# Two transformer layers on one core: row steps at five seams issued as a pipeline over token tiles, and one product cut in halves

## The chip, the core and the metric

The kernel runs on one core of a Trainium2 chip. A core has five engines that run side by side and meet only at semaphores: TensorE (PE, matrix products), VectorE (DVE), ScalarE (ACT), GpSimd (POOL) and SyncE (SP), whose queue issues nearly all of this kernel's transfers. SBUF is the working memory, PSUM the accumulator of PE. The metric is the device time of one execution in microseconds (us), the median over the timed executions. Below, "tile" with a number is one of the eight blocks of 128 tokens (tile 0 to tile 7).

## What is computed

Two layers on 1024 tokens of width 1024, all in fp32. Cut to what the change touches:

```python
# first layer, after its attention and recurrence
mix = concat([y_att, y_rwkv]) @ w_out                      # seam A
x   = x + g_m * rms_norm(mix, mix_post_norm)
hf  = rms_norm(x, ffn_pre_norm) * (1 + sc_f) + sh_f
f   = (silu(hf @ w_ffn_gate) * (hf @ w_ffn_up)) @ w_ffn_down
x   = x + g_f * rms_norm(f, ffn_post_norm)                 # seam B
# second layer
u   = rms_norm(x, g_mix_pre);  z = u @ w_in                # seam B, its end
mixed = sigmoid(gate_a) * ya + sigmoid(gate_b) * (ob @ w_b_out)
h   = x + rms_norm(mixed @ w_o, g_mix_post)                # seam C
u2  = rms_norm(h, g_ffn_pre)                               # seam C, its end
f   = (gelu(conv(u2 @ w_ffn_up)) * ...) @ w_ffn_down
h   = h + rms_norm(f, g_ffn_post)                          # seam D
g   = sigmoid(h @ w_ple_gate)
h   = h + rms_norm(e * g, g_ple_post)                      # seam E
```

rms_norm divides each token's row by the root of the mean of its squares and multiplies by a gain.

## The kernel before

Every fp32 operand of a product is kept as a high and a low part (the low one is a subtraction on DVE or POOL, called a split here), and a product takes three matmuls (`mm3`, three lines of the profile: L105 to L107 in the plain products, L288 to L290 in the feed-forward ones). Operands of products lie with the model width on the partitions, so a token row that was normalized has to be transposed by PE before the next product. The feed-forward products use seven products in place of eight for a two by two block, so the transposed rows of two token tiles are also combined into sums (`put_pair`, which ends with the transposes, ACT copies and some nine DVE operations for a pair of tiles).

A **seam** is the place where one big product ends and the next begins. There each of the eight token tiles goes through row steps of 1024 columns: sum of squares on ACT (L119), the reciprocal root on POOL (two tiny operations, L114 and L115, tile `rs_y`), the scaling by root and gain on DVE (`scalar_tensor_tensor`, L530 in `post_add`, L541 in `renorm`), the residual add on DVE (L531), a store of the new residual to DRAM, then the second norm in the same way, and the transposes with their copies and splits (L154 or the lines of `put_pair`).

- **Seam A** (`mo2`): the second half (k 0 to 3) of w_out's product, added by DVE (L1928) to a first half that was stored in DRAM earlier (`half_d`), then the row steps and `put_pair`.
- **Seam B** (`done1`): row steps after the last products of the first w_ffn_down; `done` is called for the even tiles between the last product and its sum into `acc` (L468), for the odd ones after it.
- **Seam C** (`mo3`, `mo4`): four blocks `ob` are made (load `yl`, multiply by `yr` on DVE L2020, split on ACT and POOL L215; `yl` and `yr` have one buffer each), eight feature blocks are made from them (`fm`, DVE product L2028, POOL add L2029 with a loaded `ma`, one buffer), then the whole product with w_o, eight rows of weights, for each token tile, and the row steps.
- **Seam D** (`done2`): as B after the second w_ffn_down, without the second norm. The weights of w_ple_gate are loaded behind the stores of x1d, since SP issues in order.
- **Seam E** (`pl`): the product with w_ple_gate and the last norm.

The program is written as Python loops, but the order in which an engine runs its instructions is not that of the text alone: the tile framework's scheduler (switched on by one argument at the kernel's end) gives each engine its own order by modelled times, and the semaphores follow. So some work of neighbouring token tiles already overlaps in the kernel before.

Of the kernel before, what the change touches and what calls it, by code (L numbers as in the profile page):

```python
# [8 lines left out]
FP = mybir.dt.float32  # L9
# [15 lines left out]
class Core:  # L25
# [84 lines left out]
    def rsqrt(self, x, n, scale, eps):  # L110

        nc = self.nc
        y = self.small.tile([128, n], FP, name="rs_y", tag=f"rs_y{n}")
# [104 lines left out]
class Ops:  # L218
# [28 lines left out]
    def put_pair(self, c, g, xe, xo):  # L247

        nc = c.nc
        raw = lambda: c.t2([128, 4, 128])  # L250

        def tr(x, q):
            ps = c.psum([128, 4, 128], "tr")
            for k in range(4):
                nc.tensor.transpose(ps[:, k], x[:, (4 * q + k) * 128:(4 * q + k + 1) * 128], c.ident)
            return ps

        def put(s, x, eng):
# [19 lines left out]
        put(self.S1, s1, nc.vector)  # L278
        put(self.S3, s3, nc.gpsimd)
        put(self.S2, a11, nc.vector)  # L280
        put(self.S4, a12, nc.gpsimd)


def mm7(c, out, pairs, start, stop):
# [112 lines left out]
def down7(c, ap, rings, fd, w, nk, done):  # L397
# [56 lines left out]
    ops = ahead(operands(), c.nah)  # L454
    bank = lambda: [c.psum([128, 2, 512]) for _ in range(2)]

    def mul(ps, start, *to, between=None):
        n, s, t = next(ops)
        for g in range(4):
            gs = slice(128 * g, 128 * g + 128)  # L460
            mm7(c, ps[g // 2][:, g % 2], [((s[:, 0, j, gs], s[:, 1, j, gs]), (t[:, 0, j], t[:, 1, j])) for j in range(n)], start, True)
        if between is not None:
            between()
        for e, h in to:
            for q in range(2):
                d = acc[:, 2 * q:2 * q + 2, e, 512 * h:512 * h + 512]
                if (e, h) in first:
                    nc.vector.tensor_add(d, d, ps[q])  # L468
                else:
                    nc.scalar.activation(d, ps[q], AF.Copy)  # L470
            first.add((e, h))

    for n in range(len(groups)):
        pa, pb = bank(), bank()
# [3 lines left out]
        mul(pb, False, (0, 1))  # L478
        mul(pa, False, (1, 1))
        mul(bank(), True, (0, 0))  # L480
        mul(pa, False, (1, 0), between=None if n < len(groups) - 1 else
            lambda: [done(i, acc[:, i // 2, 0]) for i in range(0, NT, 2)])
    for i in range(1, NT, 2):
        done(i, acc[:, i // 2, 1])


class Rings:
# [31 lines left out]
    return {name: cols[:, s] for name, s in at.items()}  # L519


def post_add(c, ap, y, x, G, out, t=None):

    nc = c.nc
    ss = c.small.tile([128, 1], FP, name="ss", tag="ss")
    c.sumsq(y, ss, ap.tile([128, D], BF, name="sqj", tag="sqj", bufs=1))
    r = c.rsqrt(ss, 1, 1.0 / D, EPS)
    if t is None:
        t = ap.tile([128, D], FP, name="pa", tag="s4", bufs=c.n4)
# [4 lines left out]
def renorm(c, ap, x, i, act, g, b=None):  # L534

    nc = c.nc
    ss = c.small.tile([128, 1], FP, name="ss", tag="ss")
    c.sumsq(x, ss, ap.tile([128, D], BF, name="sqj", tag="sqj", bufs=1))
    r = c.rsqrt(ss, 1, 1.0 / D, EPS)
# [1243 lines left out]
def two_layers(ctx, tc, *args):  # L1783
# [91 lines left out]
    with pool("mo") as ap:  # L1875
# [14 lines left out]
        def prologue():  # L1890
# [4 lines left out]
                features(k)  # L1895
                yield
            for i in range(NT):
                for hf in range(2):
                    sl = slice(hf * 512, hf * 512 + 512)
                    t = ap.tile([128, 512], FP, name="hm", bufs=2)  # L1900
                    ps = c.psum([128, 512])
                    c.mm3(ps, [((h.tok(k, 0, i), h.tok(k, 1, i)), (wt[k - 4][:, 0, sl], wt[k - 4][:, 1, sl])) for k in range(4, 8)])
                    nc.scalar.activation(t, ps, AF.Copy)
                    nc.sync.dma_start(half[i * 128:i * 128 + 128, sl], t)
                    yield
# [11 lines left out]
        c.wlayout()  # L1917
    at.__exit__(None, None, None)
    c.layout(ps=(2, 2), tr=(1, 4))
    with pool("mo2") as ap:  # L1920
# [3 lines left out]
        get, get_h = loader(ap, x_in), loader(ap, half, "ht", 2)  # L1924
        for i in range(NT):
            ps = row_product(c, h, wt, i, range(4))
            y = get_h(i)
            nc.vector.tensor_add(y, y, ps)  # L1928
            xt = get(i)
            post_add(c, ap, y, xt, G1, xt, y)  # L1930
            store(x1d, i, xt)
            xn = renorm(c, ap, xt, i, None, Gh, Bh)
            if i % 2:
                h.put_pair(c, i // 2, xe, xn)
            xe = xn
    wp.__exit__(None, None, None)
    fd = tc.dram_tile([22, 128, T], FP, name="f_d")
    c.layout(ps=(1, 8))
# [16 lines left out]
    with Down(c, pool, "d1") as dn:  # L1955
# [3 lines left out]
        def done1(i, y):  # L1959
# [5 lines left out]
            _, G2, Gu = h  # L1965
            with c.after():
                xt = get(i)
            post_add(c, dn.ap, y, xt, G2, y, y)
            store(x2d, i, y)
            h[0].put_T(c, i, renorm(c, dn.ap, y, i, None, Gu), "ps")  # L1970
        dn.run(fd, p["w_ffn_down"], done1)
    h = h[0]
    c.layout(ps=(2, 3), tr=(1, 2))
# [33 lines left out]
    c.layout(ps=(2, 3), tr=(1, 2))  # L2007
    hp = pool("hp2")
    h = Ops(hp.__enter__(), "h2")
    wp = ctx.enter_context(ExitStack())  # L2010
    woa = wp.enter_context(pool("woa"))
    wt = rows_w(c, woa, p["w_o_2"], range(3), "woa")
    with pool("mo3") as ap:
        ob = []
        for k in range(4):
            t = ap.tile([128, T], FP, name="yl", bufs=1)
            nc.sync.dma_start(t, obd[k])
            r = ap.tile([128, T], FP, name="yr", bufs=1)
# [12 lines left out]
    c.n4 = 3
    c.wlayout()
    c.layout(ps=(2, 2), tr=(1, 4))
    wob = wp.enter_context(pool("wob"))
    c.wlayout(2)
    wt += rows_w(c, wob, p["w_o_2"], range(3, 8), at={7: h.free(3)})
    c.wlayout()
    with pool("mo4") as ap:
        G3, Gh = row_bcast(c, ap, p["g_mix_post_2"], "G3"), row_bcast(c, ap, p["g_ffn_pre_2"], "Gh2")
        c.tp, c.nt2 = ap, 5  # L2040
        get = loader(ap, x2d)
        for i in range(NT):
            ps = row_product(c, h, wt, i)
            xt = get(i)
            post_add(c, ap, ps, xt, G3, xt)
            store(h1d, i, xt)
            xn = renorm(c, ap, xt, i, None, Gh)
            if i % 2:
                h.put_pair(c, i // 2, xe, xn)
            xe = xn  # L2050
    wp.close()
    fd = tc.dram_tile([22, 128, T], FP, name="f2_d")
    c.layout(ps=(1, 8))
    c.wlayout(4, 7)
# [7 lines left out]
    with Down(c, pool, "d2") as dn:  # L2062
# [3 lines left out]
        def done2(i, y):  # L2066
# [14 lines left out]

    c.layout(ps=(2, 4))
    c.wlayout(3, 1)
    c.n4 = 6
    with pool("pl") as ap:
        G5 = row_bcast(c, ap, p["g_ple_post_2"], "G5")
        get, get_e = loader(ap, x1d), loader(ap, ed)
        wt = rows_w(c, ap, p["w_ple_gate_2"], range(8))
        for i in range(NT):
            ps = row_product(c, h, wt, i)  # L2090
            g = ap.tile([128, D], FP, name="pg", tag="s4", bufs=c.n4)
# [4 lines left out]
            post_add(c, ap, g, xt, G5, xt, g)  # L2096
            store(out, i, xt)
    c.wlayout()
    hp.__exit__(None, None, None)

# [23 lines left out]
```

## Time and profile before

| what | value |
|---|---|
| timed executions | 3799.55, 3803.8, 3804.47 us, median 3803.8 us |
| profiled execution | 3812.14 us, of which the profile's span is 3810.3 us |
| mean granted TensorE clock | 0.862 of full speed |
| busy shares of the span | PE 86%, DVE 61%, POOL 40%, ACT 38% |

The profiled execution is one more run of the same program; times of stages are taken from it. A busy share says how long an engine had an instruction in flight, averaged over stages with different limits. Of the granted clock there are two levels, full (2.4 GHz, shown as 1.00) and half (1.2 GHz, 0.50); a stretch shows the mean of what it had.

### The profile page before, as it was taken

Reading aid. Unit: us, or ns where it says so; the run is one execution under the profiler, and the core shown is the slowest. Engines: PE = TensorE matmul, PEld = TensorE weight load, DVE = VectorE, ACT = ScalarE, POOL = GpSimd, SP = SyncE. Lnnn points to the kernel's source line nnn. Section 1 sums busy time; section 2 is a strip of 40 time slices with the busy share of each in tenths; the row PEclk is TensorE's granted clock in tenths of the full one; section 3 lists DMA queues with packets and bytes.
Section 4 is the critical chain, followed back from the end, with each engine's and each line's share of the span. In section 5 each row is a group of like instructions: output and inputs, shape, how many; then the busy total and the mean of one; then the engine's idle time right before and its main releaser. Section 6 shows DMA issues by size and latency. Waiting matters only on the chain.

```text
span 3810.3 us, 42512 instructions
## 1 busy us (share of the span) xinstructions
PE 3273.1 (86%) x15652; PEld 2637.0 (69%) x15652; DVE 2313.9 (61%) x3405; ACT 1430.9 (38%) x2433; POOL 1515.3 (40%) x1217
## 2 busy tenths in 40 slices
PE   3778767998996869999886999989978899998888
PEld 2666545676774658887675788777856688886767
DVE  5569977657643465454898110016743688888983
ACT  3345433333333243333433221136632444444332
POOL 3114345424323244443874322131133354547851
PEclk7888865556567879999997999999989899999989
DMA  5552232212123432222332222220043222213234
GB/s 172 151 167 79 85 122 67 73 39 63 36 68 119 153 105 84 83 83 71 114 125 75 80 58 89 87 77 10 7 133 138 89 83 83 83 61 138 101 138 148
DMA packets 262655, 356.15 MB, mean 93 GB/s; under 512 B 17599, under 2 KB 194720, under 8 KB 261424
## 3 DMA queue, kind: packets, MB, share of 16 engines
q1 hardware_dynamic: 261392, 353.21, 28.6%
q8 instruction: 123, 2.02, 0.2%
q14 instruction: 84, 0.69, 0.1%
q0 software_dynamic: 1056, 0.23, 0.0%
HBM read 257.36 MB, written 96.02 MB: 93 GB/s over the span
## 4 chain that ended last, share of the span: by engine, by line
PE 48%; POOL 4%; DVE 4%; DMA 4%; issue 2%; ACT 2%; SPq 0%; POOLq 0%; ACTq 0%; DVEq 0%
PE ps L288 9%; PE ps L290 9%; PE ps L289 9%; PE ps L106 5%; PE ps L105 5%; PE ps L107 5%; POOL op L437 2%; POOL sm L429 1%; DMA raw<-f_d 1%; DVE sm L429 1%; PE o L578 1%; PE tp L570 1%; ACT sqj L119 1%; PE o L105 1%; PE o L106 1%
## 5 line engine op out<-in xcount | busy, mean ns | idle before, releaser
L288 PE MATMUL ps<-h,op 128*128 128x512 f32 x1232 | 475.5, 392 | 14.4 <-ACT op L311 12.4
L290 PE MATMUL ps<-h,op 128*128 128x512 f32 x1232 | 481.0, 391 | 3.2 <-POOL op L313 3.2
L289 PE MATMUL ps<-h,op 128*128 128x512 f32 x1232 | 481.6, 391 | 0.0
L288 PE MATMUL ps<-op,op 128*128 128x512 f32 x616 | 245.8, 402 | 48.3 <-ACT op L435 31.1
L288 PEld LDWEIGHTS ps<-h,op 128*128 128x128 f32 x1232 | 232.8, 189 | 64.2 <-ACT op L311 13.2
L290 PEld LDWEIGHTS ps<-h,op 128*128 128x128 f32 x1232 | 232.6, 189 | 52.9 <-POOL op L313 4.7
L289 PEld LDWEIGHTS ps<-h,op 128*128 128x128 f32 x1232 | 232.8, 189 | 48.5
L89 POOL TENSOR_TENSOR whl<-wraw,whl 128x1024 fp32r<-128x1024 f32 (+1 forms) x62 | 127.2, 2053 | 348.9 <-ACT whl L88 345.6
L313 POOL TENSOR_TENSOR op<-t,op 128x512 fp32r<-128x512 f32 x88 | 130.3, 1480 | 322.8 <-ACT op L311 322.8
L289 PE MATMUL ps<-op,op 128*128 128x512 f32 x616 | 245.2, 399 | 7.6 <-DVE op L437 7.6
L290 PE MATMUL ps<-op,op 128*128 128x512 f32 x616 | 244.0, 398 | 3.4 <-POOL op L437 3.4
L1692 DVE TENSOR_TENSOR up<-t,ps 128x512 f32<-128x512 f32 x176 | 116.5, 683 | 166.6 <-ACT t L351 119.6
L105 PE MATMUL ps<-h,whl 128*128 128x512 f32 x512 | 203.1, 400 | 15.5 <-ACT h L214 13.5
L106 PE MATMUL ps<-h,whl 128*128 128x512 f32 x512 | 203.7, 398 | 3.1 <-POOL h L215 3.1
L351 ACT ACTIVATE t<-ps 128x512 f32<-128x512 f32 x132 | 78.4, 594 | 332.8 <-PE ps L290 332.2
L107 PE MATMUL ps<-h,whl 128*128 128x512 f32 x512 | 202.6, 396 | 0.0
L468 DVE TENSOR_TENSOR acc<-acc,ps 128x1024 f32<-128x1024 f32 x152 | 179.5, 1209 | 13.6 <-PE ps L290 13.6
L288 PEld LDWEIGHTS ps<-op,op 128*128 128x128 f32 x616 | 118.6, 193 | 80.2 <-ACT op L435 38.8
L1369 DVE SCALAR_TENSOR_TENSOR cv<-up,v_fw,cv 128x1023 f32<-128x1023 f32 x88 | 150.0, 1704 | 32.0 <-ACT cv L1367 31.1
L578 PE MATMUL o<-pT,v 128*128 128x256 f32 (+1 forms) x640 | 155.3, 361 | 14.3 <-ACT pT L573 9.1
L114 POOL TENSOR_SCALAR rs_y<-ss 128x1 f32<-128x1 f32 (+2 forms) x90 | 33.2, 368 | 330.7 <-ACT sqj L119 265.7
L573 ACT ACTIVATE pT<-tp 128x512 fp32r<-128x512 f32 (+2 forms) x221 | 94.4, 445 | 183.2 <-PE tp L570 146.6
(589 smaller groups left out, 8652.7 us busy)
## 6 DMA issues: line engine op xcount, KB each, us to landing
wraw<-in_w_ffn_up_dram SPq DMA_DIRECT2D x66, 512.0 KB, 3.9
adaw<-in_ada_w_dram SPq DMA_DIRECT2D x96, 256.0 KB, 3.5
raw<-in_w_ffn_down_dram SPq DMA_DIRECT2D x44, 512.0 KB, 6.8
raw<-f_d SPq DMA_DIRECT2D x44, 512.0 KB, 5.3
wraw<-in_w_in_dram SPq DMA_DIRECT2D x42, 512.0 KB, 3.9
wraw<-in_w_ffn_gate_dram SPq DMA_DIRECT2D x22, 512.0 KB, 3.9
f_d<-up SPq DMA_DIRECT2D x22, 512.0 KB, 2.8
f_d<-cv SPq DMA_DIRECT2D x22, 512.0 KB, 2.6
```

The source lines that it names most:

```text
L89: self.nc.gpsimd.tensor_sub(hl[:, 1], raw, hl[:, 0].bitcast(FP))
L105: self.nc.tensor.matmul(out, lh, rh, start=first and i == 0, stop=False)
L106: self.nc.tensor.matmul(out, lh, rl, start=False, stop=False)
L107: self.nc.tensor.matmul(out, ll, rh, start=False, stop=last and i == n - 1)
L288: mm(out, lh, rh, start=start and i == 0, stop=False, skip_group_check=True)
L289: mm(out, lh, rl, start=False, stop=False, skip_group_check=True)
L290: mm(out, ll, rh, start=False, stop=stop and i == n - 1, skip_group_check=True)
L313: (nc.gpsimd if n[0] % 2 else nc.vector).tensor_sub(t[:, 1], x, t[:, 0].bitcast(FP))
L468: nc.vector.tensor_add(d, d, ps[q])
L578: nc.tensor.matmul(o[:, q], v[:, b0 + s].rearrange("p a d -> p (a d)"), pT[:, x, s, q], start=b0 == 0 and n == 0, stop=end and n == 3)
L1369: nc.vector.scalar_tensor_tensor(out[:, s:], ps[:, :T - s], w[2 - s][:, j:j + 1], out[:, s:], op0=ALU.mult, op1=ALU.add)
L1692: nc.vector.tensor_add(halves(x[j])[e], tok(a), tok(b))
```

## The change

A new function `pipeline` takes one generator per token tile, and lets each of those begun go one step further, the oldest last, after a new one was begun. The row steps are cut into such steps by `yield`: product, first sum and statistics, `post_add` and second statistics, `renorm`, transposes. In seams B and D the residual add goes from VectorE to GpSimd (`eng`). In seam C the product with w_o is cut in halves as in seam A: the half with k 0 to 3 is made for two tiles at a time in the last four iterations of the loop that makes the features and stored in `half2_d`, the half with k 4 to 7 is made afterwards and added to it. `yl` and `ms` share two buffers, `yr` and `ma` one; the feature loop's add goes from GpSimd to VectorE.

```diff
-    def mul(ps, start, *to, between=None):
+    def mul(ps, start, *to):
...
-        mul(pa, False, (1, 0), between=None if n < len(groups) - 1 else
-            lambda: [done(i, acc[:, i // 2, 0]) for i in range(0, NT, 2)])
-    for i in range(1, NT, 2):
-        done(i, acc[:, i // 2, 1])
+        if n < len(groups) - 1:
+            mul(pa, False, (1, 0))
+    mul(pa, False)
+
+    def end(i):
+        if i == 1:
+            add(pa, 1, 0)
+        yield from done(i, acc[:, i // 2, i % 2])
+    pipeline(end(i) for i in (0, 2, 4, 6, 1, 3, 5, 7))
...
+def post_add(c, y, r, x, G, out, t, eng=None):
...
     nc.vector.scalar_tensor_tensor(t, y, r, G, op0=ALU.mult, op1=ALU.mult)
-    nc.vector.tensor_add(out, t, x)
+    (eng or nc.vector).tensor_add(out, t, x)
...
+def pipeline(gens):
+
+    active, gens = [], iter(gens)
+    more = True
+    while more or active:
+        g = next(gens, None)
+        more = g is not None
+        if more:
+            active.insert(0, g)
+        active = [g for g in active if next(g, active) is not active]
...
+    def mixed(i, ap, h, wt, ks, get_h, get, dst, G, g, b=None):
+
+        ps = row_product(c, h, wt, i, ks)
+        yield
+        y, xt = get_h(i), get(i)
+        nc.vector.tensor_add(y, y, ps)
+        r = stats(c, ap, y)
+        yield
+        post_add(c, y, r, xt, G, xt, y)
+        store(dst, i, xt)
+        r = stats(c, ap, xt)
+        yield
+        xns[i] = renorm(c, ap, xt, r, g, b)
+        yield
+        if i % 2:
+            yield from h.put_pair(c, i // 2, xns[i - 1], xns[i])
...
-            t = ap.tile([128, T], FP, name="yl", bufs=1)
+            t = ap.tile([128, T], FP, name="yl", tag="ms", bufs=2)
...
         for m in range(8):
+            ps = fm(c, c.split_w(c.load_cols(p["w_b_out_2"], m * 128, 128, 4)), 4, ob)
+            for i in range(2 * m - 8, 2 * m - 6):
+                if i >= 0:
+                    for _ in half_product(ap, h, list(enumerate(wt)), i, half):
+                        pass
...
+        wt += [rows(k) for k in range(4, 8)]
...
+            post_add(c, y, r, xt, G4, y, y, nc.gpsimd)
```

**The order on VectorE in seam B.** In the kernel before, VectorE's rows from the sums into `acc` on; `acc` holds all token tiles, and L530, L531, L154 and L541 are the first scaling, the residual add, the low part of the transposed row and the second scaling.

```order
L530 SCALAR_TENSOR_TENSOR acc_13147<-acc_13147,rs_y_14641,G2_14599 128x1024
L531 TENSOR_TENSOR acc_13147<-acc_13147,xt_14636 128x1024
L154 TENSOR_TENSOR h1_14598<-ps_14622,h1_14598 128x4x128
L154 TENSOR_TENSOR h1_14598<-ps_14629,h1_14598 128x4x128
L541 SCALAR_TENSOR_TENSOR xn_14653<-acc_13147,rs_y_14650,Gu_14601 128x1024
L530 SCALAR_TENSOR_TENSOR acc_13147<-acc_13147,rs_y_14674,G2_14599 128x1024
L531 TENSOR_TENSOR acc_13147<-acc_13147,xt_14669 128x1024
```

In the changed kernel the same place on VectorE (the first scaling is now L541, the second L549):

```order
L549 SCALAR_TENSOR_TENSOR xn_14645<-acc_13147,rs_y_14625,Gu_14601 128x1024
L541 SCALAR_TENSOR_TENSOR acc_13147<-acc_13147,rs_y_14633,G2_14599 128x1024
L549 SCALAR_TENSOR_TENSOR xn_14664<-acc_13147,rs_y_14642,Gu_14601 128x1024
L541 SCALAR_TENSOR_TENSOR acc_13147<-acc_13147,rs_y_14652,G2_14599 128x1024
L154 TENSOR_TENSOR h1_14598<-ps_14666,h1_14598 128x4x128
L154 TENSOR_TENSOR h1_14598<-ps_14673,h1_14598 128x4x128
L154 TENSOR_TENSOR h1_14598<-ps_14701,h1_14598 128x4x128
L154 TENSOR_TENSOR h1_14598<-ps_14708,h1_14598 128x4x128
```

The adds are gone from VectorE, and two tiles take their turns together.

**The order on GpSimd in seam D.** Before, GpSimd had only the pairs L114 and L115 there. In the changed kernel, after the last splits of w_ffn_down and the first add, it has these rows (L542 is the residual add):

```order
L542 TENSOR_TENSOR acc<-acc,xt 128x1024
L115 TENSOR_TENSOR rs_y<-rs_y,mhalf 128x1
L114 TENSOR_SCALAR rs_y<-ss 128x1 x2
L542 TENSOR_TENSOR acc<-acc,xt 128x1024
L115 TENSOR_TENSOR rs_y<-rs_y,mhalf 128x1 x2
L114 TENSOR_SCALAR rs_y<-ss 128x1
L542 TENSOR_TENSOR acc<-acc,xt 128x1024
L114 TENSOR_SCALAR rs_y<-ss 128x1
L115 TENSOR_TENSOR rs_y<-rs_y,mhalf 128x1
L542 TENSOR_TENSOR acc<-acc,xt 128x1024 x2
L115 TENSOR_TENSOR rs_y<-rs_y,mhalf 128x1
L542 TENSOR_TENSOR acc<-acc,xt 128x1024 x2
```

The adds (the last seven of eight are shown) now stand in GpSimd's queue between the roots that the scalings wait for, and the eight splits of the w_ple_gate rows stand behind the last of them.

**The order of transfers on SP in seam C.** In the changed kernel, at the end of the feature loop (L1909 stores 512 of the 1024 columns of a token tile's first half, sixteen stores in all, L82 loads a row of w_o, k = 7, L1733 the gains, L1820 the reloads of the halves and of x2d):

```order
L1909 DMA half2_d_20315<-hm_20875 128x512
L1909 DMA half2_d_20315<-hm_20891 128x512
L1909 DMA half2_d_20315<-hm_20907 128x512
L82 DMA wraw_20946<-in_w_o_2_dram 128x1024
L1733 DMA G3_20960<-in_g_mix_post_2_dram 128x1024
L1733 DMA Gh2_20962<-in_g_ffn_pre_2_dram 128x1024
L1820 DMA xt_21014<-half2_d_20315 128x1024
L1820 DMA xt_21016<-x2d_77 128x1024
```

The last row of w_o, the gains and the reloads now stand behind the last store of the halves; there were no such stores before.

## Rows read from the trace of the kernel before

**Rows 1.** The page, its first part: busy time, share of the span, instructions.
```profile
PE 3273.1 (86%) x15652; PEld 2637.0 (69%) x15652; DVE 2313.9 (61%) x3405; ACT 1430.9 (38%) x2433; POOL 1515.3 (40%) x1217
```

**Rows 2.** Busy time by stretch: length, PE, PEld, DVE, ACT, POOL, clock, DMA.
```profile
1285.77:1374.87 89.10, 47.84 (x205) 38.20 (x203) 76.14 (x76) 38.20 (x71) 30.44 (x39) 0.75 0.44 148
2049.31:2101.23 51.92, 17.40 (x75) 13.72 (x73) 39.64 (x40) 25.61 (x44) 15.72 (x30) 0.57 0.44 151
2773.79:2833.93 60.14, 38.93 (x182) 27.64 (x181) 25.46 (x62) 25.27 (x53) 22.93 (x12) 0.75 0.52 161
2833.93:2887.10 53.17, 45.01 (x180) 36.29 (x180) 18.08 (x16) 10.97 (x13) 24.56 (x13) 0.92 0.46 153
2887.10:2912.47 25.37, 18.55 (x62) 13.01 (x63) 1.22 (x1) 6.14 (x7) 12.60 (x7) 0.82 0.36 124
2912.47:3004.49 92.02, 77.29 (x370) 64.35 (x368) 54.81 (x61) 38.99 (x71) 27.51 (x38) 0.93 0.33 109
3674.16:3700.47 26.31, 15.57 (x67) 11.62 (x65) 25.86 (x28) 12.97 (x23) 12.41 (x14) 0.64 0.40 154
3708.61:3799.30 90.69, 90.25 (x384) 73.88 (x384) 25.94 (x21) 23.96 (x29) 24.09 (x22) 0.96 0.47 162
```

**Rows 3.** Timeline, seam A: start, length, engine, instruction, idle before and releaser.
```profile
1313.42 3.58 POOL L261 TENSOR_TENSOR h<-t,h 128x512 fp32r<-128x512 f32 x2
1313.56 2.30 DVE L543 TENSOR_TENSOR xn<-xn,Bh 128x1024 f32<-128x1024 f32 x1
1371.86 1.26 POOL L261 TENSOR_TENSOR h<-t,h 128x512 fp32r<-128x512 f32 x1 [7.20 <-ACT h L260]
1375.51 0.79 PE L288 MATMUL ps<-h,op 128*128 128x512 f32 x1 [6.19 <-ACT op L311]
```

**Rows 4.** Timeline, seam B.
```profile
2067.43 1.28 DVE L541 SCALAR_TENSOR_TENSOR xn<-acc,rs_y,Gu 128x1024 f32<-128x1024 f32 x1 [1.01 <-POOL rs_y L115]
2069.44 1.28 DVE L530 SCALAR_TENSOR_TENSOR acc<-acc,rs_y,G 128x1024 f32<-128x1024 f32 x1 [0.72 <-POOL rs_y L115]
2071.90 1.28 DVE L154 TENSOR_TENSOR h<-ps,h 128x512 fp32r<-128x512 f32 x2
2074.20 1.28 DVE L541 SCALAR_TENSOR_TENSOR xn<-acc,rs_y,Gu 128x1024 f32<-128x1024 f32 x1 [1.01 <-POOL rs_y L115]
2097.79 1.22 DVE L531 TENSOR_TENSOR acc<-acc,xt 128x1024 f32<-128x1024 f32 x1
2099.46 9.56 SPq L77 DMA_DIRECT2D wraw<-in_w_in_dram  x4
2102.66 1.94 PE L151 MATMUL ps<-ident,xn 128*128 128x128 f32 x8 [4.82 <-DVE xn L541]
2106.23 0.80 PE L105 MATMUL ps<-h,whl 128*128 128x512 f32 x1 [1.63 <-ACT whl L88]
```

**Rows 5.** Timeline, seam C.
```profile
2806.76 2.35 POOL L215 TENSOR_TENSOR h<-yl,h 128x1024 fp32r<-128x1024 f32 x1 [9.27 <-ACT h L214]
2809.14 0.33 SPq L2017 DMA_DIRECT2D yl<-obd  x1
2812.61 1.23 DVE L2020 TENSOR_TENSOR yl<-yl,yr 128x1024 f32<-128x1024 f32 x1 [9.81 <-DMA yl<-obd]
2831.58 2.35 POOL L215 TENSOR_TENSOR h<-yl,h 128x1024 fp32r<-128x1024 f32 x1 [5.92 <-ACT h L214]
3004.49 0.80 PE L288 MATMUL ps<-h,op 128*128 128x512 f32 x1 [6.19 <-ACT op L311]
```

**Rows 6.** Timeline, seams D and E.
```profile
3678.79 0.19 POOL L114 TENSOR_SCALAR rs_y<-ss 128x1 f32<-128x1 f32 x1
3679.07 0.55 POOL L115 TENSOR_TENSOR rs_y<-rs_y,mhalf 128x1 f32<-128x1 f32 x1
3699.25 1.22 DVE L531 TENSOR_TENSOR acc<-acc,xt 128x1024 f32<-128x1024 f32 x1
3708.61 2.01 PE L105 MATMUL ps<-wo,h 128*128 128x512 f32 x4 [3.82 <-ACT wo L1379]
```

More of the change, by code (lines that the diff above doesn't have):

```diff
@@ L112, in rsqrt @@
         nc = self.nc
-        y = self.small.tile([128, n], FP, name="rs_y", tag=f"rs_y{n}")
+        y = self.small.tile([128, n], FP, name="rs_y", tag=f"rs_y{n}", bufs=8 if n == 1 else None)
         nc.gpsimd.tensor_scalar(y, x, scale, eps, op0=ALU.mult, op1=ALU.add)
@@ L278, in put_pair @@
         put(self.S1, s1, nc.vector)
+        yield
+        put(self.S2, a11, nc.vector)
         put(self.S3, s3, nc.gpsimd)
-        put(self.S2, a11, nc.vector)
         put(self.S4, a12, nc.gpsimd)
+        yield
 def mm7(c, out, pairs, start, stop):
@@ L455, in down7, with add @@
     bank = lambda: [c.psum([128, 2, 512]) for _ in range(2)]
-    def mul(ps, start, *to, between=None):
+    def add(ps, e, h):
+        for q in range(2):
+            d = acc[:, 2 * q:2 * q + 2, e, 512 * h:512 * h + 512]
+            if (e, h) in first:
+                nc.vector.tensor_add(d, d, ps[q])
+            else:
+                nc.scalar.activation(d, ps[q], AF.Copy)
+        first.add((e, h))
+    def mul(ps, start, *to):
         n, s, t = next(ops)
@@ L461, in mul @@
             mm7(c, ps[g // 2][:, g % 2], [((s[:, 0, j, gs], s[:, 1, j, gs]), (t[:, 0, j], t[:, 1, j])) for j in range(n)], start, True)
-        if between is not None:
-            between()
         for e, h in to:
[L465 to L471, printed above, removed]
+            add(ps, e, h)
     for n in range(len(groups)):
@@ L519, in vectors, with stats, renorm @@
     return {name: cols[:, s] for name, s in at.items()}
-def post_add(c, ap, y, x, G, out, t=None):
-    nc = c.nc
[L525 to L529, printed above, removed]
+def stats(c, ap, x):
+    ss = c.small.tile([128, 1], FP, name="ss", tag="ssp", bufs=8)
+    c.sumsq(x, ss, ap.tile([128, D], BF, name="sqj", tag="sqj", bufs=1))
+    return c.rsqrt(ss, 1, 1.0 / D, EPS)
+def post_add(c, y, r, x, G, out, t, eng=None):
+    nc = c.nc
     nc.vector.scalar_tensor_tensor(t, y, r, G, op0=ALU.mult, op1=ALU.mult)
-    nc.vector.tensor_add(out, t, x)
-def renorm(c, ap, x, i, act, g, b=None):
+    (eng or nc.vector).tensor_add(out, t, x)
+def renorm(c, ap, x, r, g, b=None):
     nc = c.nc
-    ss = c.small.tile([128, 1], FP, name="ss", tag="ss")
-    c.sumsq(x, ss, ap.tile([128, D], BF, name="sqj", tag="sqj", bufs=1))
-    r = c.rsqrt(ss, 1, 1.0 / D, EPS)
     t = ap.tile([128, D], FP, name="xn", tag="s4", bufs=c.n4)
@@ L1863, in store, with half_product @@
         nc.sync.dma_start(dst[i * 128:(i + 1) * 128], x)
+    xns = [None] * NT
+    def mixed(i, ap, h, wt, ks, get_h, get, dst, G, g, b=None):
[4 more added lines that the diff above has]
+        r = stats(c, ap, y)
+        yield
+        post_add(c, y, r, xt, G, xt, y)
+        store(dst, i, xt)
+        r = stats(c, ap, xt)
+        yield
+        xns[i] = renorm(c, ap, xt, r, g, b)
+        yield
+        if i % 2:
+            yield from h.put_pair(c, i // 2, xns[i - 1], xns[i])
+    def half_product(ap, h, wt, i, dst):
+        for hf in range(2):
+            sl = slice(hf * 512, hf * 512 + 512)
+            t = ap.tile([128, 512], FP, name="hm", bufs=2)
+            ps = c.psum([128, 512])
+            c.mm3(ps, [((h.tok(k, 0, i), h.tok(k, 1, i)), (w[:, 0, sl], w[:, 1, sl])) for k, w in wt])
+            nc.scalar.activation(t, ps, AF.Copy)
+            nc.sync.dma_start(dst[i * 128:i * 128 + 128, sl], t)
+            yield
     while next(attend, True) is not True:
@@ L1897, in prologue @@
             for i in range(NT):
[L1898 to L1905, printed above, removed]
+                yield from half_product(ap, h, list(zip(range(4, 8), wt)), i, half)
                 if i < 4:
@@ L1923, in two_layers @@
         c.tp, c.nt2 = ap, 5
[L1924 to L1935, printed above, removed]
+        pipeline(mixed(i, ap, h, wt, range(4), loader(ap, half, "ht", 2), loader(ap, x_in), x1d, G1, Gh, Bh) for i in range(NT))
     wp.__exit__(None, None, None)
@@ L1967, in done1 @@
                 xt = get(i)
-            post_add(c, dn.ap, y, xt, G2, y, y)
+            r = stats(c, dn.ap, y)
+            yield
+            post_add(c, y, r, xt, G2, y, y, nc.gpsimd)
             store(x2d, i, y)
-            h[0].put_T(c, i, renorm(c, dn.ap, y, i, None, Gu), "ps")
+            r = stats(c, dn.ap, y)
+            yield
+            u = renorm(c, dn.ap, y, r, Gu)
+            yield
+            h[0].put_T(c, i, u, "ps")
         dn.run(fd, p["w_ffn_down"], done1)
@@ L2009, in two_layers @@
     h = Ops(hp.__enter__(), "h2")
-    wp = ctx.enter_context(ExitStack())
-    woa = wp.enter_context(pool("woa"))
-    wt = rows_w(c, woa, p["w_o_2"], range(3), "woa")
+    c.wlayout(2, 3)
+    wp = pool("woa")
+    woa = wp.__enter__()
+    half = tc.dram_tile([T, D], FP, name="half2_d")
+    rows = lambda k: rows_w(c, woa, p["w_o_2"], [k], "woa", 5)[0]
+    wt = [rows(k) for k in range(4)]
     with pool("mo3") as ap:
@@ L2040, in two_layers @@
         c.tp, c.nt2 = ap, 5
[L2041 to L2051, printed above, removed]
+        pipeline(mixed(i, ap, h, wt, range(4, 8), loader(ap, half, "ht", 2), loader(ap, x2d), h1d, G3, Gh) for i in range(NT))
+    wp.__exit__(None, None, None)
     fd = tc.dram_tile([22, 128, T], FP, name="f2_d")
@@ L2088, in two_layers, with ple @@
         wt = rows_w(c, ap, p["w_ple_gate_2"], range(8))
-        for i in range(NT):
+        def ple(i):
             ps = row_product(c, h, wt, i)
+            yield
             g = ap.tile([128, D], FP, name="pg", tag="s4", bufs=c.n4)
@@ L2095, in two_layers @@
             xt = get(i)
-            post_add(c, ap, g, xt, G5, xt, g)
+            r = stats(c, ap, g)
+            yield
+            post_add(c, g, r, xt, G5, xt, g)
             store(out, i, xt)
+        pipeline(ple(i) for i in range(NT))
     c.wlayout()
```

23 lines of the change are left out of this document (10 added, 13 removed).

## The prediction

> **What bounds the kernel now.** I read the shares first: TensorE is busy 86% of the span [rows 1]. So a change elsewhere pays only where TensorE stands, and the granted clock shows where that is. Then I cut the seams out as stretches [rows 2]. In seam A (first row) VectorE is busy 76.14 of 89.10 us and TensorE 47.84. In seam B (second) VectorE 39.64 of 51.92, TensorE 17.40 at a mean clock of 0.57. Seam C is four rows: making the four blocks, the feature loop, a gap of 25.37 us in which the rows of w_o are got ready, and the product with its row steps, where TensorE is busy 77.29 of 92.02. In seam D (seventh row) VectorE is busy 25.86 of 26.31: it has no gap. In seam E (last) TensorE is busy 90.25 of 90.69, so no order of row steps can shorten it; E is worth 0.
>
> Last I read, in the timeline, what ends VectorE's waits. In B each token tile has two, 1.01 and 0.72 us, both ended by the root on GpSimd [rows 4], and the tiles follow each other every 74.20 − 67.43 = 6.77 us: 5.04 of work and 1.73 of waits. Those waits are a chain of one tile (sum of squares, root, scaling) with nothing put in between.
>
> **Seam A.** The same 76 VectorE operations, in another order; nothing is removed. What can be won is the idle time, 89.10 − 76.14 = 12.96 us [rows 2]. Pipelining lets a neighbour fill it, except at the start and in the last tile, which has no neighbour; I take half, a gain of 7 (0 to 12). The up product starts at 1375.51 [rows 3], when the last pair is transposed and combined, so VectorE's end moves it one for one. The transposes of the last pair and SP's loads behind the last store move with it.
>
> **Seam B.** VectorE loses the add and keeps two scalings (one every 1.2, half of a pair of neighbouring operations) and two splits (1.28 together, [rows 4]): about 3.8 a tile. GpSimd gets the add. No row shows this add on GpSimd; the nearest is its subtraction of the same shape, 2.35 [rows 5], against 1.22 on VectorE [rows 4]. With two roots of 0.19 + 0.55 [rows 6] GpSimd has 3.85 a tile. The two engines also hinder each other: in seam A a VectorE add, undisturbed 1.22 [rows 4], took 2.30 beside two GpSimd operations of 1.26 that took 3.58 in place of 2.52 [rows 3]. Each lost about 1.1, as if they took turns. An add also waits for its scaling, and behind it in GpSimd's queue stand the roots of the next tiles, for which VectorE's scalings wait. If one scaling per tile falls on an add, GpSimd needs 3.85 + 1.2 = 5.05 a tile, and sets the pace. The gain is (6.77 − 5.05) × 8 = 13.8, less about 4 to fill a pipeline of two tiles: 10. The end is w_in's product, at 2106.23, which follows the last add (2097.79 + 1.22), its store and the loads behind it [rows 4]; store and loads wait for GpSimd now, in the same order. Bounds: no contention and no fill, 14; everything in turns, below, 4; I let it fall to 0.
>
> **Seam C.** Three parts.
>
> The four blocks: the first split starts at 2806.76, the last at 2831.58 [rows 5], 3 × 8.27 apart, because yl has one buffer: its next load (2809.14) comes only after the split, and 3.5 us pass until VectorE multiplies (2812.61). With two buffers the second load stands ready and two more overlap. From load to multiply 3.5, multiply 1.2, from there to the next split, by the rest of the 8.27, 1.2 (the copy on ACT), split 2.35: the third block is split by 2817.4, the fourth (its yr has one buffer and waits for the third multiply) by about 2823.2, against 2833.9. Gain 10.7 at that point.
>
> The loop: TensorE is busy 45.01 of 53.17 there [rows 2], held by loads of ma. The changed loop adds eight half products of 24 × 0.235 = 5.6 (90.25 us for 384 matmuls, last of [rows 2]), so it becomes TensorE's: 45 for features and 45 for halves, less the about 8 that the earlier start already lets it do, 82 from 2823, or 2905. VectorE gets the adds (8 × 1.2) and ACT sixteen copies of half the columns (0.6 each, half of that copy); VectorE has 18.08 and ACT 10.97 busy in 53.17 [rows 2], so both are covered. The sixteen stores and eight reloads find the transfer engines at 0.33 to 0.46 [rows 2].
>
> The rest: w_o's row 7 is queued behind the last store of a half (the order above), and the gains, reloads and x2d behind it. Loaded from 2905.4 in 3.5, copied in 1.2, split in 2.35, and about 1 for the queue, it is there at 2913.5; with 3.5 for the first tile's last matmuls and their sum (an estimate) VectorE's first row step is at 2917. From there VectorE is the bound, no longer TensorE: it had 54.81 of work [rows 2], and gets eight adds of the halves, 64.5; with waits as I leave them in A and B, 9 more, it ends at 2917 + 73.5 = 2990.5 against 3004.49 [rows 5]. Gain 14 (0 if the second half runs as the whole did, 18 if row 7 comes at once).
>
> **Seam D.** Here the move costs. VectorE is relieved of 8 × 1.2, but GpSimd needs 8 × (2.35 + 0.74) = 24.7 from the first scaling's end at about 3675.4: 3700.1 if nothing disturbs it, which is where VectorE ended before (3699.25 + 1.22, [rows 6]). Each scaling that falls on an add lengthens it; eight of them make 9.6. I take half: a loss of 5 (0 to 9). x1d's stores wait for the adds, w_ple_gate's loads stand behind those stores, and TensorE's first product (3708.61, [rows 6]) waits for them, so all of the 5 arrives at the end.
>
> **Sum.** −7 − 10 − 14 + 5 = −26. The profiled execution took 3812.14 with a span of 3810.3, 8.3 above the median of 3803.8; I subtract from the median: 3778.
>
> **A rule against it.** The Trainium skill, "GPSIMD Engine Reference", section "Engine selection", advises against elementwise work of two inputs on GpSimd, about twice as slow as on VectorE; 2.35 against 1.22 agrees. "SBUF — State Buffer", section "Who interferes with whom", says that a VectorE instruction with two SBUF inputs and a GpSimd one that reads SBUF share a port that the first to start holds for its whole length, while the other stands. The row of [rows 3] (2.30 in place of 1.23) agrees. By that rule the sum would be the −16 of the first rival, by the half that I took −26.
>
> **Rivals.** (1) *Full turns.* Every scaling in B and D excludes the add. B then needs 2.35 + 2 × 1.2 + 1.48 = 6.2 a tile: gain 4 (8 × 0.54). D loses 9. Sum −7 − 4 − 14 + 9 = −16: 3788. For it speak [rows 3]; against it, that the splits of L154, which read PSUM, are a third of VectorE's time there, and adds can fall beside those.
>
> (2) *Already overlapped.* The scheduler had put neighbours between each other in A (76 of 89 busy), so A gives 1, and in C a late row 7 or late reloads leave only 3. Sum −1 − 10 − 3 + 5 = −9: 3795.
>
> (3) *Slower: TensorE at the half clock in C's second half.* TensorE would be busy about 6.6 of 9.2 us a tile there, in bursts; in A, at 47.84 of 89.10, the mean clock was 0.75 [rows 2]. At half clock a tile needs 24 × 0.47 = 11.3 and 1.94 for eight transposes [rows 4], 13.2, more than VectorE's 9.2. Some 7.6 tiles from 2913.5 end at 3014. The tail from the last product to the up product is, in the kernel before, about 13 (92.02 less seven eighths of 90.25, [rows 2]), so that it starts at 3027, a loss of 22: −7 − 10 + 22 + 5 = +10, 3814. It decides if the clock stays at 0.50 for most of the stretch. Against it: TensorE would then never stand, and in E, where it never stands, the clock was 0.96.
>
> (4) *All of it.* Upper ends everywhere, D at 0: −44, 3760.
>
> **Chances.** Forecast 0.45, full turns 0.20, already overlapped 0.15, half clock 0.06, all of it 0.14. The range reaches from near the last to beyond the second rival: 3762 to 3801. Runs of this kernel tell about 0.2%, 7.6 us, from no change. Below 3796 lie the forecast, the fourth and first rivals nearly whole and half of the second: faster 0.83; same 0.10, slower 0.07.
>
> **What would show it.** A: VectorE's idle time in the row steps falls from 13 to about 6, and the up product starts 7 earlier. B: tiles every 5 us or so, L542 on GpSimd at 2.4 to 3.6; if its mean is above 3.5 the first rival holds. C: last split of a block near 2823, TensorE busy from there to 2905 at clock 1.00, VectorE's first add at 2917 less what A and B gave, the stretch then VectorE's. D: the last add ends some 30 us after the first scaling, and E's first matmul comes 8 after it. E: unchanged, 90.7. I would be wrong most easily in C, if reloads of halves or row 7 come later than the queue's order suggests, or in A, if the waits that remain are those of the transposes.

## The result, and the profile after

The changed kernel took 3831.57 us in the median of six executions (3827.62 to 3841.23), the kernel before 3807.19 (3799.55 to 3819.55). The ratio is 1.0062, with a 95% interval of 1.004 to 1.0085: slower by some 24 us, where a gain of 26 was forecast. The profiled execution was the longest of the six, 3841.23 us with a span of 3839.5.

First, the busy time by stretch of the changed kernel, with the columns of [rows 2]: seam A, seam B to w_in's first matmul, then C as blocks, feature loop, gap and row steps, then D to w_ple_gate's first matmul, and E.

```profile
1286.47:1369.50 83.03, 49.06 (x209) 39.87 (x209) 74.97 (x78) 39.91 (x73) 38.09 (x40) 0.73 0.47 162
2055.04:2107.93 52.89, 19.79 (x83) 15.75 (x81) 40.91 (x35) 26.02 (x45) 40.60 (x38) 0.58 0.44 152
2816.71:2837.13 20.42, 10.58 (x30) 6.83 (x30) 2.45 (x2) 4.12 (x4) 9.41 (x4) 0.82 0.46 154
2837.13:2919.48 82.35, 79.82 (x332) 64.54 (x333) 32.38 (x24) 19.80 (x28) 11.11 (x6) 0.96 0.47 160
2919.48:2939.91 20.43, 16.39 (x59) 12.27 (x58) 0.00 (x1) 4.77 (x6) 7.11 (x3) 0.83 0.68 243
2939.91:3014.52 74.61, 46.84 (x222) 38.26 (x220) 64.23 (x69) 39.67 (x73) 32.52 (x40) 0.82 0.49 161
3697.00:3738.14 41.14, 18.93 (x84) 14.83 (x82) 26.65 (x27) 16.96 (x29) 30.33 (x22) 0.62 0.46 163
3738.14:3828.54 90.40, 90.02 (x383) 73.87 (x384) 26.07 (x21) 23.96 (x29) 24.04 (x22) 0.96 0.46 162
```

The seams alone do not explain the result. Cut between the same instructions in every profile (A from the first add of a half to the first up matmul, B and D from the first scaling to the next product's first matmul, C from the store of the last block to the second layer's first up matmul), the whole execution divides like this, in us. The last two columns are of experiments told below:

| stretch | before | changed | distance restored | before, tiles moved |
|---|---|---|---|---|
| start to A | 1283.2 | 1286.5 | 1270.2 | 1270.1 |
| A | 92.3 | 83.0 | 81.6 | 92.2 |
| feed-forward 1, not edited | 673.8 | 685.5 | 673.3 | 684.5 |
| B | 56.9 | 52.9 | 53.0 | 56.9 |
| w_in to last block, not edited | 696.6 | 708.8 | 701.1 | 704.3 |
| C | 201.7 | 197.8 | 196.8 | 204.1 |
| feed-forward 2, not edited | 669.7 | 682.5 | 670.7 | 680.0 |
| D | 34.5 | 41.1 | 41.4 | 34.5 |
| E and tail | 101.7 | 101.4 | 101.4 | 101.6 |

The seams gave −9.2 − 4.0 − 3.9 + 6.7 = −10.4. The three long stretches between them, in which no instruction was edited, lost 11.7 + 12.2 + 12.8 = 36.7. The stretch ahead of A differs by up to 16 us between executions whatever the kernel, and is left out of what follows.

In those three stretches TensorE runs the same number of matmuls in both kernels and stands idle for about as long (96 us of 2040 before, 97 of 2077 now), at a mean clock of 0.97 to 0.98 in each. What grew is its busy time, from 1943.6 to 1979.5. The sums over the three stretches, before and changed (us, then busy time by engine):

```profile
sum 2040.07, PE 1943.63 PEld 1605.13 DVE 1223.83 ACT 777.54 POOL 921.63; mean PE 647.88 PEld 535.04 DVE 407.94 ACT 259.18 POOL 307.21
sum 2076.80, PE 1979.52 PEld 1614.53 DVE 1230.10 ACT 778.96 POOL 920.23; mean PE 659.84 PEld 538.18 DVE 410.03 ACT 259.65 POOL 306.74
```

Inside them lie parts in which TensorE is never idle and its clock is granted in full. The same 200 us of the first up product, before (TensorE's count is the first number in brackets):

```profile
1500.00:1700.00 200.00, 200.00 (x884) 165.65 (x883) 100.30 (x111) 68.34 (x112) 80.35 (x57) 1.00 0.27 86
```

And in the changed kernel:

```profile
1500.00:1700.00 200.00, 200.00 (x862) 162.20 (x861) 95.65 (x107) 67.61 (x111) 79.96 (x56) 1.00 0.25 81
```

The same busy time holds 884 matmuls before and 862 after: one every 226.7 ns, and now one every 232.4 (by the start times; 200 us over the counts give 226.2 and 232.0). A share of busy time cannot show this, and neither can a wait. Counting the matmuls in a stretch does, or comparing the busy time of the same matmuls.

**What had moved.** The compiled programs give the cause to test. The change also has these lines, which add buffers to two tiny tiles:

```diff
-        y = self.small.tile([128, n], FP, name="rs_y", tag=f"rs_y{n}")
+        y = self.small.tile([128, n], FP, name="rs_y", tag=f"rs_y{n}", bufs=8 if n == 1 else None)
...
+    ss = c.small.tile([128, 1], FP, name="ss", tag="ssp", bufs=8)
```

`rsqrt`'s tile went from four to eight buffers and the new `stats` tile has eight; each takes 32 bytes of a partition, so everything allocated after them on the left side of SBUF lies 12 × 32 = 384 bytes further. Weights and their split parts are for the most part in pools on the right side, which did not move. In the compiled programs `h` begins at byte 23520 of a partition before and at 23904 now, and the first buffer of `op` at 200672 in both. Products with one operand from each side (`h` and `h2` with `op`; `hT`, `h1`, `h2` and `yain` with `whl`; 6096 matmuls in all) had their operands a multiple of 256 bytes apart before, and 128 off a multiple now. Products with both operands from one side (w_ffn_down, w_ple_gate, w_o) kept their distance, and there the spacing stayed at about 227. 6096 × 5.7 ns = 35 us. Of the 6096, 5232 lie in the three stretches, which makes 30 of their 36.7; the rest is about what these stretches differ by from one execution to the next (5 us in the third column of the table).

### The profile page after: what moved, and what is told of

Read it like the earlier page. It is cut to its first block, busy times and chain, and to the rows that moved or that the text cites. A ratio compares the mean times of both kernels' runs of the same rounds, so it can differ in the third digit from the quotient of the medians.

```text
span 3839.5 us, 42553 instructions
## 1 busy us (share of the span) xinstructions
PE 3302.8 (86%) x15652; PEld 2644.5 (69%) x15652; DVE 2332.9 (61%) x3405; ACT 1438.6 (37%) x2449; POOL 1550.2 (40%) x1225
## 4 chain that ended last, share of the span: by engine, by line
PE 60%; DVE 16%; DMA 8%; POOL 7%; issue 5%; ACT 3%; SPq 1%; DVEq 0%; POOLq 0%; ACTq 0%
PE ps L291 9%; PE ps L293 9%; PE ps L292 9%; PE ps L105 5%; PE ps L107 5%; PE ps L106 5%; DVE junk L845 3%; PE o L596 2%; POOL op L440 2%; PE tp L588 2%; POOL sm L432 2%; DVE tmp L1225 1%; PE xy L1289 1%; DMA raw<-f_d 1%; DMA adaw<-in_ada_w_dram 1%
## 5 line engine op out<-in xcount | busy, mean ns | idle before, releaser
L291 PE MATMUL ps<-h,op 128*128 128x512 f32 x1232 | 481.8, 397 | 14.4 <-ACT op L314 12.5
L293 PE MATMUL ps<-h,op 128*128 128x512 f32 x1232 | 486.9, 396 | 3.2 <-POOL op L316 3.2
L292 PE MATMUL ps<-h,op 128*128 128x512 f32 x1232 | 487.4, 396 | 0.0
L596 PE MATMUL o<-pT,v 128*128 128x256 f32 (+1 forms) x640 | 156.3, 363 | 17.0 <-ACT pT L591 10.4
L438 ACT ACTIVATE op<-sm 128x1024 fp32r<-128x1024 f32 (+1 forms) x96 | 91.5, 982 | 189.3 <-POOL sm L432 89.0
```

The costliest lines, as they stand in the source:

```text
L291: mm(out, lh, rh, start=start and i == 0, stop=False, skip_group_check=True)
L292: mm(out, lh, rl, start=False, stop=False, skip_group_check=True)
L293: mm(out, ll, rh, start=False, stop=stop and i == n - 1, skip_group_check=True)
L596: nc.tensor.matmul(o[:, q], v[:, b0 + s].rearrange("p a d -> p (a d)"), pT[:, x, s, q], start=b0 == 0 and n == 0, stop=end and n == 3)
```

## The experiments

**1. The distance restored.**

```diff
-    ss = c.small.tile([128, 1], FP, name="ss", tag="ssp", bufs=8)
+    ss = c.small.tile([128, 1], FP, name="ss", tag="ssp", bufs=12)
```

> The changed kernel, with twelve in place of eight buffers for the tiny tile of the row sums. Everything that is allocated after those tiny tiles then lies 512 bytes further in each partition than in the kernel before, in place of 384. Theory 1 (place in SBUF): in the changed kernel the products whose two operands lie in pools of the two sides stand 384 bytes apart from where they stood to each other, and their matmuls come every 232.4 ns in place of 226.7 (some 5900 of them: 5900 x 5.7 ns = 34 us); with 512 bytes they come every 226.7 again, the stretches that were not edited are as long as before, and the time falls by about 34 us to some 3797, 10 below the kernel before. Theory 2 (the longer unedited stretches are scatter between executions, or the transfers of the new buffer in DRAM): the spacing stays near 232 and the time near 3831.

Measured: 3798.24 us, ratio to the kernel before 0.9974 (0.9957 to 0.9992); the kernel before, run again beside it, took 3811.0. The same 200 us of this run:

```profile
1500.00:1700.00 200.00, 200.00 (x885) 165.58 (x884) 99.52 (x111) 70.13 (x115) 80.74 (x57) 1.00 0.25 80
```

885 matmuls again, and the unedited stretches are back to within 5 us (table above, third column); TensorE's busy time in them is 1945.1, where it was 1943.6 before and 1979.5 in the changed kernel. Four more tiny buffers, with no instruction changed, take 33 us away. What is left, some 10 us below the kernel before, agrees with the sum of the seams, some −12 in its profile.

**2. The distance broken in the kernel before.** The same edit at the three places that make this tile:

```diff
-    ss = c.small.tile([128, 1], FP, name="ss", tag="ss")
+    ss = c.small.tile([128, 1], FP, name="ss", tag="ss", bufs=8)
```

> The kernel before, with eight in place of four buffers for one tiny tile, which moves all later tiles by 128 bytes; nothing else. Theory 1: the matmuls of the same products come every 232.4 ns, seams A to E keep their lengths but for that, and the time is about 34 us longer, some 3841. Theory 2: 3807, as before.

Measured: 3843.6 us, ratio 1.0088 (1.006 to 1.0116), 33 us slower, with seams A, B, D and E as before and C 2.4 us longer:

```profile
1500.00:1700.00 200.00, 200.00 (x863) 162.13 (x862) 97.41 (x108) 70.60 (x116) 82.24 (x58) 1.00 0.25 79
```

TensorE's busy time in the three unedited stretches is 1974.8. Scatter and the new DRAM buffer are ruled out: this kernel has none of the change but four more tiny buffers, and with them a displacement of 128 bytes, and it loses what the changed kernel lost. More buffers by themselves are not the cause either, since experiment 1 has still more of them and is fast.

**3. The distance by itself.** One program with two arrays of operands, and groups of 60 matmuls that differ only in a displacement:

```python
s, m = 128 * (j % 32) + ds // 4, 512 * (j % 8) + dm // 4
nc.tensor.matmul(ps, st[:, s:s + 128], mv[:, m:m + 512], ...)
```

> Not the two layers: groups of 60 matmuls of 128x512, each with its own weights, one operand moved by some bytes in each partition against the other from group to group; the output holds sums of these products. By the theory that the distance of the two operands' places counts, the spacing is about 227 ns at a distance of 0, 256, 512 and 1024 bytes and about 232 at 128 and 384, whichever operand is moved, and 227 where both are moved by the same. What 32, 64, 96, 160, 192 and 224 do no run has shown. If absolute places count, the groups with both moved by 64 or 128 differ from 227 too; if neither counts, all groups have one spacing.

One execution of 314.07 us. Windows of it from a group's first matmul to the next group's. In order: the moving operand displaced by 0, 32, 64, 128, 256 and 384 bytes, then the weights by 128, then both by 128.

```profile
50.46:64.06 13.60, 13.60 (x61) 11.26 (x60) 0.69 (x2) 0.00 (x0) 0.00 (x0) 1.00 0.00 0
64.06:78.06 14.00, 14.00 (x61) 11.24 (x60) 0.69 (x2) 0.00 (x0) 0.00 (x0) 1.00 0.01 1
78.06:91.81 13.75, 13.75 (x61) 11.27 (x60) 0.69 (x2) 0.00 (x0) 0.00 (x0) 1.00 0.00 0
105.82:119.82 14.00, 14.00 (x61) 11.26 (x60) 0.69 (x2) 0.00 (x0) 0.00 (x0) 1.00 0.00 0
161.87:175.49 13.62, 13.62 (x61) 11.27 (x60) 0.68 (x2) 0.00 (x0) 0.00 (x0) 1.00 0.00 0
175.49:189.48 13.99, 13.99 (x61) 11.26 (x60) 0.69 (x2) 0.00 (x0) 0.00 (x0) 1.00 0.01 1
230.69:244.64 13.95, 13.95 (x61) 11.30 (x60) 0.69 (x2) 0.00 (x0) 0.00 (x0) 1.00 0.00 0
285.62:299.20 13.58, 13.35 (x59) 10.70 (x57) 0.63 (x2) 0.00 (x0) 0.00 (x0) 1.00 0.00 0
```

Sixty matmuls take 13.6 us at a distance of 0 or 256, 13.75 at 64, 14.0 at 32, 128 and 384 (13.95 where the weights are displaced by 128), and 13.6 when both are displaced alike. It is the distance that counts, and a distance of 256 counts as none.

**4. The adds back on VectorE** (with the distance restored; halves and pipelining stay).

```diff
-            post_add(c, y, r, xt, G2, y, y, nc.gpsimd)
+            post_add(c, y, r, xt, G2, y, y)
...
-            post_add(c, y, r, xt, G4, y, y, nc.gpsimd)
+            post_add(c, y, r, xt, G4, y, y)
```

> The changed kernel with the 512 byte shift, and with the residual adds of seams B and D back on VectorE; the pipelining and the halves of seam C stay. If GpSimd's adds and VectorE's scalings take turns (in the changed kernel a scaling beside an add took 3.36 us in place of 1.28, and B went at 6.36 us a tile), B falls to about 5.1 us a tile (8 x 1.2 = 10 less) and D loses its 6.7: some 3781. If the roots on GpSimd were the bound there, B and D stay as they are: 3797.

Measured: 3792.01 us, ratio 0.9944 (0.9923 to 0.9965); this is 11 us less than with GpSimd's adds, by the two ratios, where 16 were expected. Seam B took 46.8 us in place of 53.0, and D 34.5 in place of 41.4. The changed kernel's timeline shows how the adds cost, in B:

```profile
2081.40 2.34 POOL L542 TENSOR_TENSOR acc<-acc,xt 128x1024 f32<-128x1024 f32 x1
2084.90 2.35 POOL L542 TENSOR_TENSOR acc<-acc,xt 128x1024 f32<-128x1024 f32 x1 [1.16 <-DVE acc L541]
...
2068.74 3.36 DVE L541 SCALAR_TENSOR_TENSOR acc<-acc,rs_y,G 128x1024 f32<-128x1024 f32 x1 [0.72 <-POOL rs_y L115]
...
2081.47 3.36 DVE L541 SCALAR_TENSOR_TENSOR acc<-acc,rs_y,G 128x1024 f32<-128x1024 f32 x1 [0.72 <-POOL rs_y L115]
2084.75 2.47 DVE L154 TENSOR_TENSOR h<-ps,h 128x512 fp32r<-128x512 f32 x4
```

The add began at 2081.40, the scaling 0.07 later; the add kept its 2.34, and the scaling took 3.36 in place of 1.28, so that it ended about 1.1 after the add. The one that began first was not held up at all. A pair of tiles took 2081.47 − 2068.74 = 12.73, or 6.37 a tile. The four splits L154 beside the second add (2084.90) kept their length, 2.47 for four against 1.28 for two before [rows 4]; one of their two inputs lies in PSUM. With the adds on VectorE the same place runs so:

```profile
2047.13 1.28 DVE L549 SCALAR_TENSOR_TENSOR xn<-acc,rs_y,Gu 128x1024 f32<-128x1024 f32 x1 [0.44 <-POOL rs_y L115]
2049.13 1.28 DVE L541 SCALAR_TENSOR_TENSOR acc<-acc,rs_y,G 128x1024 f32<-128x1024 f32 x1 [0.72 <-POOL rs_y L115]
2050.33 1.22 DVE L542 TENSOR_TENSOR acc<-acc,xt 128x1024 f32<-128x1024 f32 x1
...
2057.91 1.28 DVE L549 SCALAR_TENSOR_TENSOR xn<-acc,rs_y,Gu 128x1024 f32<-128x1024 f32 x1 [0.44 <-POOL rs_y L115]
```

A pair takes 2057.91 − 2047.13 = 10.78 us, 5.39 a tile, with more work on VectorE. In D of the changed kernel GpSimd held the end:

```profile
3713.36 3.27 POOL L542 TENSOR_TENSOR acc<-acc,xt 128x1024 f32<-128x1024 f32 x1
3717.50 5.65 POOL L542 TENSOR_TENSOR acc<-acc,xt 128x1024 f32<-128x1024 f32 x2
3727.13 2.35 POOL L542 TENSOR_TENSOR acc<-acc,xt 128x1024 f32<-128x1024 f32 x1 [1.17 <-DVE acc L541]
3738.16 18.85 POOL L1398 TENSOR_TENSOR wo<-wraw,wo 128x1024 fp32r<-128x1024 f32 x8 [8.68 <-ACT wo L1397]
```

**5. Seam C: late row, halves, pipelining.** Three kernels, all with the adds on VectorE. First, row 4 of w_o in place of rows 5 to 7:

```diff
-        wt += [rows(k) for k in range(4, 8)]
+        wt += [rows(4)] * 4
```

> As the run with the adds back on VectorE, but the rows k = 5 to 7 of w_o are neither loaded nor split: row 4 stands in for them, so that the second half of that product is another one. If the late last row is what TensorE and VectorE wait for between the feature loop and the row steps (20.4 us from the last feature to VectorE's first add), that gap falls by about 8 us, to 12, and seam C to 189. If the reloads of the halves or the gains come as late as the row, it stays at 19 to 20.

One execution, 3780.89 us, read by its profile. The gap from the last feature to VectorE's first add was 14.56 us in place of 20.4, and in it TensorE was never idle:

```profile
2881.32:2895.88 14.56, 14.56 (x66) 12.07 (x65) 0.00 (x1) 1.72 (x3) 0.00 (x0) 1.00 0.63 199
```

The late rows cost 6, not 8, and without them C still took 192.9, where 189 was expected. Second and third, the halves taken out again (two buffers for the blocks and the feature loop's add on VectorE stay), once with the row steps pipelined and once tile after tile:

```diff
+        pipeline(whole(i) for i in range(NT))
```

> As the run with the adds back on VectorE, but seam C with w_o's product whole, as in the kernel before, its row steps pipelined, and the two shared buffers for the loaded blocks kept. If the halves are what eats the gain of the earlier blocks (the last of eight rows of w_o comes late and TensorE stands 8 us, and the row steps then wait for VectorE), seam C takes about 191 us from the last store of obd to the up product, against 198 with halves and 202 before: 7 less than the run with the adds back. If the halves pay, it is longer by up to 10.

```diff
-        pipeline(whole(i) for i in range(NT))
+        for i in range(NT):
+            ps = row_product(c, h, wt, i)
...
+            xt = get(i)
```

> As the run with the adds back on VectorE, but seam C with w_o's product whole and its row steps issued tile after tile, as in the kernel before; of the change C keeps only the shared buffers for the loaded blocks and the feature loop's add on VectorE. In the run with the whole product and pipelined steps the row part of C took 105.66 us against 92.01 before. If pipelining with only three row buffers did that, the row part is 92 again and C is 21 + 49 + 25 + 92 = 187 us, 10 less than with halves: some 3782. If the whole product is slow there for another reason (the order of the weights), it stays near 202 and 3790.

The pipelined one took 3790.58 us (0.9955, 0.9939 to 0.9971) and its C 202.6: no gain, against the 191 that I expected. The waits of VectorE in its row part say why (what waited and for whom, total, times, longest):

```profile
DVE pa L541 <- PE tr L255: 38.4, 5, 16.8
DVE pa L541 <- POOL rs_y L115: 30.5, 2, 27.2
```

The scaling waited for transposes of another tile, that is, by the code, for a row buffer to come free: with all eight rows of w_o in SBUF there are three, shared by the loaded rows and the results of both scalings. In the sequential kernel, with three as well, no scaling waited for a transpose. That more buffers would make the pipeline pay was not tried. The sequential one took **3775.91 us, ratio 0.991 (0.9892 to 0.9929)**, the fastest of all kernels run. Its C, as blocks, loop, gap and row part:

```profile
2774.67:2795.28 20.61, 11.42 (x30) 7.70 (x30) 2.45 (x2) 4.12 (x4) 9.40 (x4) 0.71 0.48 153
2795.28:2843.33 48.05, 43.55 (x180) 35.48 (x180) 31.05 (x24) 10.90 (x12) 5.69 (x5) 0.93 0.56 181
2843.33:2871.09 27.76, 20.74 (x63) 14.72 (x64) 0.00 (x2) 6.29 (x7) 12.48 (x7) 0.73 0.32 113
2871.09:2962.98 91.89, 77.20 (x369) 64.28 (x367) 54.84 (x61) 38.97 (x71) 27.50 (x38) 0.93 0.34 109
```

188.3 in place of 197.0 with halves, where 187 was expected: the halves lengthen the loop by 33 us (81.1 against 48.05), and with the pipelined row steps they give back 17 in the row part and 7 in the gap.

## Why the prediction was wrong, point by point

**The sum.** The step that failed is that the sum had terms for the five seams only and put the rest at nothing, without a reason. The rest lost some 33 us (35 by the count of matmuls) through the displacement of one operand against the other, which the diff causes by `bufs=8` in two places; the prediction asks nowhere what these buffers move. Experiments 1 and 2 show the cause, with both signs; 3 shows it apart from the kernel. Without it the changed kernel is at 0.9974, some 10 us below the kernel before. So 16 of the 26 would be missing even then: 6 in B, 10 in C and 2 in D, with 2 more than forecast from A.

**A**, forecast −7, measured −9.2 (−10.7 with the distance restored). The mechanism was right: VectorE is busy 74.97 of 83.03, so 8.1 us idle are left. Cut from the same add, the kernel before had 14.3:

```profile
1283.25:1375.51 92.26, 49.09 (x209) 39.21 (x209) 77.96 (x78) 39.94 (x74) 30.97 (x40) 0.75 0.44 146
```

So 6.2 came from filled waits, as forecast, and 3.0 because VectorE's own work fell from 77.96 to 74.97: in the main because three L543 adds of 2.3 beside GpSimd's operations (one stands in [rows 3]) took 1.2 in the new order. That part was luck.

**B**, forecast −10, measured −4.0, the number of the first rival. My term let one scaling per tile lengthen the add on GpSimd, with the roots at 0.74 each. Measured, the add was hardly lengthened there (2.34 to 2.39) and a scaling was, from 1.28 to 3.36, so VectorE's chain carried the cost. The sign I named for it, a mean of L542 above 3.5, looked at the wrong engine. The roots were mis-sized too: beside a scaling the first operation of a root took 1.28, where [rows 6] has 0.19, and VectorE's next scaling waited 0.72 for that root.

```profile
2077.52 1.28 POOL L114 TENSOR_SCALAR rs_y<-ss 128x1 f32<-128x1 f32 x1
```

The wait of 0.72 in the kernel before is of the same kind (there the first operation took 0.96 beside the scaling of 2074.20), so a neighbour's scaling put beside a root brings such a wait as well as filling one. With the adds back on VectorE (experiment 4) the pipelining alone gave B 10.1, from 56.9 to 46.8: what B lacks of the forecast is the price of the move to GpSimd. The first rival's 6.2 a tile is close to the measured 6.37 partly by luck: it let every scaling exclude the add, and only one of the four scalings of a pair met one. The Trainium skill ("SBUF — State Buffer", "Who interferes with whom") says that the one that starts first holds the port for its whole instruction and the other blocks; the 2.34 and 3.36 here agree with it.

**C**, forecast −14, measured −3.9. The blocks gave their 10.7 exactly (20.42 against 31.1). The row part took 74.61, forecast 73.5. The loop was mis-sized: I had TensorE 82 us from the last block to the last half, with a credit of 8 for work already done by then. The stores show the end of it, and row 7 behind them:

```profile
2900.81 24.97 SPq L1909 DMA_DIRECT2D half_d<-hm  x8
2926.31 0.33 SPq L82 DMA_DIRECT2D wraw<-in_w_o_dram  x1
...
2931.61 2.35 POOL L1398 TENSOR_TENSOR woa<-wraw,woa 128x1024 fp32r<-128x1024 f32 x1 [2.98 <-ACT woa L1397]
...
2939.91 1.22 DVE L1890 TENSOR_TENSOR xt<-xt,ps 128x1024 f32<-128x1024 f32 x1 [20.43 <-PE ps L107]
```

From 2837.13 the last store was issued at 2925.78, after 88.6 in place of 82: TensorE stood 2.5 us of it, at a mean clock of 0.96. VectorE began 6 us after row 7 was split (2933.96), where I had 3.5. There TensorE, which had just stood twice for 1.7 us until a row of w_o was there, ran eleven matmuls at half the clock:

```profile
2934.01:2938.87 4.86, 4.86 (x11) 3.84 (x12) 0.00 (x0) 0.00 (x0) 0.00 (x0) 0.50 0.99 394
```

That is about 0.43 us each where 0.23 is usual in this kernel, some 2.3 us. The loop's 6.6 and these 2.5 are 9 of the 10 us that are missing; the row part has the last one.

**D**, forecast +5, measured +6.7: GpSimd carried the end, as forecast, with the last add done 32.5 us after the first scaling began (forecast some 30). But only two of the eight adds were lengthened, to 3.3, some 2 us in all where I had 5; the rest lies in roots that took longer beside a scaling, as in B, and in waits for scalings. So the nearness of the number is partly luck. **E**, forecast 0, measured −0.3. The half-clock rival did not come: in C's row part the mean clock was 0.82, and half the clock was seen for some 5 us in the gap.

## What to carry to other kernels

Look at the addresses when a change adds or drops even tiny buffers, and count matmuls per stretch in work that was not edited: here four 32-byte buffers decided 33 us, three times what five rewritten seams gave. Before a product is cut in halves to fill an idle engine, compare the work with the idle time of the loop that it moves into: here the loop had 8 us for 44 of work (192 matmuls of 0.23), and seam C was 9 us shorter with the product whole and its row steps tile after tile. An add moved to GpSimd was not free of VectorE here, where both read SBUF: whichever came second waited, and in B that was the engine on the chain.

## What the runs showed of the hardware

At the full granted clock, 128x512 matmuls with a weight load each came every 226.7 ns when the places of moving operand and weights differed by a multiple of 256 bytes, 229.0 with the moving operand 64 further (and with the weights 192 further, which is the same distance modulo 256), and 232.5 to 234.2 at 32, 96, 128, 160, 192, 224 and 384 (means by the start times of a group's sixty matmuls; in the two-layer kernels a distance of 128 gave 232.4). The Trainium skill's page "SBUF — State Buffer", section "Who interferes with whom", gives TensorE two read ports, one for each operand, and has it wait for nobody. The measured 3% show that TensorE's pace does depend on where its two operands lie to each other; the measurement decides. That it is the two reads which meet is not shown, and why 256 and not another number is open: no run here looked at a smaller step than 32 bytes or at other operand types.
